# Six instead of four output tiles with the first norm, and the shift's modulation on GpSimd and ScalarE

## The chip, the cores and the metric

The kernel runs on one NeuronCore of a Trainium2 chip. The metric is the device time of one execution in microseconds (us). The engines are TensorE (PE in the profile; PEld is its weight load), VectorE (DVE), ScalarE (ACT), GpSimd (POOL) and SyncE (SP), which here only issues transfers.

## The reference

The program is three layers deep: a block of RWKV-7 and convolution with its feed-forward layer, a forgetting-attention layer and an HGRN2 layer, each with a feed-forward layer behind it. The sequence has 512 tokens and the model 1,024 channels, all in float32. The change touches only the beginning:

```python
mod = jax.nn.silu(c) @ ada_w[l] + ada_b[l]
sh_m, sc_m, gt_m, sh_f, sc_f, gt_f = jnp.split(mod[:, None, :], 6, axis=-1)
h = rms_norm(x, mix_pre_g[l]) * (1.0 + sc_m) + sh_m
p = h @ w_in
p_conv, p_rw = p[..., :2 * CONV_WIDTH], p[..., 2 * CONV_WIDTH:]
prev = jnp.pad(p_rw, ((0, 0), (1, 0), (0, 0)))[:, :-1]
p_rw = p_rw + (prev - p_rw) * rwkv_mu
r, k, v, wd, ad, gd = jnp.split(p_rw, RWKV_SPLITS, axis=-1)
```

So x is normed, scaled per channel by 1 + sc_m (the scale) and moved by sh_m (the shift); both come from a matrix-vector product of `silu(c)` with a 1024x6144 matrix. The result is multiplied by `w_in`.

## The kernel before, in words

Channels lie on the 128 partitions, so the 1,024 channels are eight K tiles of 128x512. A matrix product in float32 precision is made of three: each operand is split into a rounded high part and the low rest, and hi x hi, lo x hi and hi x lo are added up in one accumulator bank of PSUM. The weight of an output tile of 128 channels (128x1024, 512 KB) is loaded to a staging buffer (tile `ws`, three of them), copied by ScalarE to its high part (L168) and subtracted by VectorE to its low part (L169); that is `wload`, L161.

`start` (L332) is the first stage. It squares x and sums it on TensorE (L340, L865), and takes the modulation of each K tile in two: q = 0 is the shift, q = 1 the scale. For K tile 0 TensorE makes both sums (L372). For K tiles 1 to 7 the tile of the transposed matrix (128x1024, one output channel per partition) is loaded by SP (`load`, L360) into one of eight borrowed rooms, and VectorE multiplies it with the broadcast vector `cb` and sums along the row, one instruction of 128x1024 for each q (L375, tiles `ada` and `NM`), then adds the bias (L376). The loads of K tile i + 4 are issued behind the modulation of K tile i.

The loop at L389 then goes over the K tiles. For each, VectorE makes the factor (L393), scales x (L394), ScalarE makes the high part with the shift as bias (L396), VectorE the low part (L397), and TensorE multiplies this K tile into four output tiles at once (L399 to L403): w and a's inputs (number 20), k, r and v of head pair 0 (12, 8, 16). Their accumulators are four banks of PSUM, open over the whole loop. Behind the loop the four are evacuated by `shift_mix` (L408: ScalarE writes a scaled copy, VectorE adds the shifted one).

`mix` (L422) calls `start` at L437 and goes on with `pair(0)` and `pair(1)` (L475). `pair` makes the missing k, r and v tiles of its head pair by `win` (L463, one output tile after the other), then `wkv_prep` (L583), which ends in small score products (L660, L673, L675). `wkv_inverse` (L686) works on GpSimd in 30 small steps (L705, L707) and through DRAM, `wkv_tail` (L765) finishes a pair. The convolution's inputs (`conv_in`, L486) and the gates (L469) are further output tiles of `w_in`. 24 more modulation tiles (L511, `ada_tile`, tile `wa`) are put at the lowest priority.

The order on each engine is not the program's: a scheduler orders the instructions when the kernel is built, by priority (the program's order) and by modelled times; on the chip each engine follows that fixed order and waits on semaphores. Tiles of one tag share their buffers, and a new tile of the tag waits until the old one has been read.

Of the kernel before, what the change touches and what calls it, by code (L numbers as in the profile page):

```python
# [9 lines left out]
F32 = mybir.dt.float32  # L10
F32R = mybir.dt.float32r
# [3 lines left out]
AF = mybir.ActivationFunctionType  # L15
# [4 lines left out]
P = 128  # L20
D = 1024
KD = 8
T1 = 512
# [53 lines left out]
MULT, ADD, SUB = ALU.mult, ALU.add, ALU.subtract  # L77
# [60 lines left out]
def bank(k, ch, *shape):  # L138
    return k.ps[ch].tile([P, *(shape or (512,))], F32, name="s" + ch)
# [21 lines left out]
def wload(k, src, nk, m=P, view=False, hl=None):  # L161

    nc = k.nc
    n = nk * m
    st = k.wst.tile([P, KD * P], F32, name="ws")
    nc.sync.dma_start(st.rearrange("p (n m) -> p n m", m=P) if view else st[:, :n], src)
    hi, lo = hl or [k.whl.tile([P, KD * P], F32R, name=q) for q in ("wh", "wl")]
    nc.scalar.copy(hi[:, :n], st[:, :n])  # L168
    nc.vector.tensor_sub(lo[:, :n], st[:, :n], hi[:, :n])  # L169
    return hi, lo  # L170


def run(steps):
    for _ in steps:
        pass
# [75 lines left out]
def split(k, hi, lo, x):  # L251
    k.nc.scalar.copy(hi, x)  # L252
    k.nc.vector.tensor_sub(lo, x, hi)
# [58 lines left out]
def silu_c(k, pool, sg):  # L312

    nc = k.nc
    k.cb = pool.tile([P, D], F32, name="cb")
    nc.scalar.dma_start(k.cb, k.A["c"].to_broadcast([P, D]))
    nc.scalar.activation(sg, k.cb, AF.Tanh, scale=0.5)
    nc.vector.scalar_tensor_tensor(k.cb, sg, 1.0, k.cb, ADD, MULT)
# [13 lines left out]
def start(k, p1, p2, first):  # L332


    nc, vec = k.nc, k.vec
    mm = nc.tensor.matmul
    x = k.h[:, :, META:T2]
    sq = squares(p2, None, "tmp", T1)
    for i in range(KD):
        add_square(k, sq, i, 0, x[:, i], T1, True)  # L340
    rs = p2.tile([P, T1], F32, name="rs", tag="k2", bufs=1)
    silu_c(k, p1, p2.tile([P, D], F32, name="sgc", tag="tok", bufs=2))
    cs = p1.tile([P, 2 * KD], F32, name="cs")
    sc = cs[:, KD:]
    nc.scalar.activation(cs[:, :KD], vec("c"), AF.Tanh, scale=0.5)
    nc.vector.scalar_tensor_tensor(sc, cs[:, :KD], 1.0, vec("c"), ADD, MULT)
    n = [0]

    def room():
        j = n[0] % 8  # L350
        n[0] += 1
        if j >= 5:
            return k.S.NM[(j - 5) // 2].rearrange("p a b c -> p (a b c)")[:, KD * P * (j % 2):KD * P * (j % 2 + 1)]
        tag, bufs = (("Dm", 1), ("Dt", 1), ("wa", 1), ("tok", 2), ("tok", 2))[j]
        return p2.tile([P, KD * P], F32, name="ada", tag=tag, bufs=bufs)

    ga = p1.tile([P, KD], F32, name="ga")
    ps = bank(k, "b", 2)

    def load(i):  # L360
        rooms[i] = []
        for q in range(2):
            rooms[i].append(room())
            nc.sync.dma_start(rooms[i][q], k.A["ada_w_t"][q] if i == 0 else k.A["ada_wT"][KD * q + i])

    def modulate(i):
        for q in range(2):
            st, nt = rooms[i][q], KD * q + i
            mod = k.mod[:, nt:nt + 1]
            if i == 0:  # L370
                for n in range(KD):
                    mm(ps[:, q:q + 1], st[:, n * P:(n + 1) * P], sc[:, n:n + 1], start=n == 0, stop=n == KD - 1)  # L372
                nc.vector.scalar_tensor_tensor(mod, ps[:, q:q + 1], 0.5, vec("ada_b", nt), MULT, ADD)
            else:
                nc.vector.scalar_tensor_tensor(st, st, 0.5, k.cb, MULT, MULT, accum_out=mod)  # L375
                nc.vector.tensor_add(mod, mod, vec("ada_b", nt))  # L376

    W, rooms = [], {}
    rms_scale(k, sq, 0, T1, rs, True)
    O = [bank(k, c) if c else k.psd.tile([P, 512], F32, name="mm") for c in ("", "", "a", "b")]  # L380
    for w in (1, 0, 2, None, None, 3, None, None):
        if w is not None:
            load(w)
            continue
        i = len(W)
        nt = first[i][0]
        W.append(wload(k, k.A["w_in_t"][nt], KD) if i < 2 else wload(k, k.A["w_in_t"][nt], KD, hl=[
            p2.tile([P, KD * P], F32R, name=f"{q}{i}", tag=q, bufs=2) for q in ("ar", "X")]))
    for i in range(KD):  # L389
        modulate(i)  # L390
        if i + 4 < KD:
            load(i + 4)
        nc.vector.scalar_tensor_tensor(ga[:, i:i + 1], k.mod[:, KD + i:KD + i + 1], 1.0, vec("mix_pre_g", i), ADD, MULT)  # L393
        nc.vector.scalar_tensor_tensor(x[:, i], x[:, i], ga[:, i:i + 1], rs, MULT, MULT)  # L394
        hi, sh = k.x1h[:, i], k.mod[:, i:i + 1]
        nc.scalar.activation(hi, x[:, i], AF.Identity, bias=sh)  # L396
        nc.vector.scalar_tensor_tensor(k.x1l[:, i], x[:, i], sh, hi, ADD, SUB)  # L397
        w = slice(i * P, (i + 1) * P)
        for (h, l), o in zip(W, O):  # L399
            xh, xl = k.x1h[:, i], k.x1l[:, i]  # L400
            mm(o, h[:, w], xh, start=i == 0, stop=False)
            mm(o, l[:, w], xh, start=False, stop=False)
            mm(o, h[:, w], xl, start=False, stop=i == KD - 1)  # L403
    for (nt, evac), o in zip(first, O):
        evac(0, o)


def shift_mix(k, ps, out, nt, m=P):  # L408

    nc = k.nc  # L410
    nc.scalar.activation(out, ps[:m], AF.Copy, scale=k.mu1[:m, nt:nt + 1])
    o = out[:, 1:]
    nc.vector.scalar_tensor_tensor(o, ps[:m, 0:T1 - 1], k.vec("rwkv_mu", nt)[:m], o, MULT, ADD)
# [8 lines left out]
def mix(k):  # L422
    tc, nc, A, vec = k.tc, k.nc, k.A, k.vec
    with ExitStack() as ctx:
        banks(k, ctx, "m", a=3, b=3)
        p1 = ctx.enter_context(tc.tile_pool(name="mx1", bufs=1))
        p2 = ctx.enter_context(tc.tile_pool(name="mx2", bufs=4))
        pd = ctx.enter_context(tc.tile_pool(name="mxd", bufs=1, space=bass.MemoryType.DRAM))
        S = k.S = K()
# [4 lines left out]
        S.wd = p1.tile([P, T1], F32, name="wd")  # L434
        tl0 = [p2.tile([P, T1], F32, name=n, bufs=3 if n == "vx" else 2) for n in ("kx", "rx", "vx")]
        mixed = lambda t, nt: (nt, lambda j, ps: shift_mix(k, ps, t, nt - 8))
        start(k, p1, p2, [mixed(S.wd, 20), mixed(tl0[0], 12), mixed(tl0[1], 8), mixed(tl0[2], 16)])  # L437
        nc.scalar.activation(S.wd[0:64], S.wd[0:64], AF.Tanh)
        S.ka1 = p1.tile([P, 4], F32, name="ka1")
        nc.vector.tensor_scalar(S.ka1, vec("k_a"), -1.0, 1.0, MULT, ADD)  # L440
# [22 lines left out]
        def win(nt, evac):  # L463
            dense(k, A["w_in_t"][nt], k.x1h, k.x1l, SEG1, evac)
# [8 lines left out]
            sigmoid(k, S.gd1, S.gd1)  # L473

        def pair(p):  # L475
            tl = tl0 if p == 0 else []
            for nt, name in ((12 + p, "kx"), (8 + p, "rx"), (16 + p, "vx")):
                if p:
                    t = p2.tile([P, T1], F32, name=name, bufs=3 if name == "vx" else 2)
                    win(*mixed(t, nt))  # L480
                    tl.append(t)
            return wkv_prep(k, p, *tl)
# [365 lines left out]
def squares(pool, acc="ssq", tmp="hf", width=T2, apool=None, **kw):  # L848

    sq = K()  # L850
    sq.apool = apool or pool
    sq.pool, sq.acc, sq.tmp, sq.width, sq.kw = pool, acc, tmp, width, kw
    return sq


def add_square(k, sq, i, c, x, n, pe=False):

    nc = k.nc
    tmp = lambda: sq.pool.tile([P, max(n, H2 + 8)], F32, name="nsq", tag=sq.tmp, **sq.kw)[:, :n]
    if pe:  # L860
        t = tmp()
        nc.scalar.activation(t, x, AF.Square)
        if i == 0:
            sq.ps = bank(k, "a")
        nc.tensor.matmul(sq.ps[:, :n], k.mean, t, start=i == 0, stop=i == KD - 1)  # L865
        return
    if i == 0 and c == 0:
        sq.sum = sq.apool.tile([P, sq.width], F32, name="ssq", tag=sq.acc, bufs=1)
    s = sq.sum[:, c:c + n]
    if i == 0:  # L870
        nc.scalar.activation(s, x, AF.Square)
        return
    t = tmp()
    nc.scalar.activation(t, x, AF.Square)
    nc.vector.tensor_add(s, s, t)


def rms_scale(k, sq, c, n, out, pe=False):

    nc = k.nc  # L880
    if not pe:
        sq.ps = bank(k, "a")
        nc.tensor.matmul(sq.ps[:, :n], k.mean, sq.sum[:, c:c + n], start=True, stop=True)
    s = sq.ps[:, :n]
    y, y2 = (sq.pool.tile([P, max(n, H2 + 8)], F32, name="rsq", tag=sq.tmp, **sq.kw)[:, :n] for _ in range(2))
    newton(k, s, y2, out, 1e-6, k.eps, y)
# [418 lines left out]
def hgrn(k):  # L1305
    tc, nc, A, vec = k.tc, k.nc, k.A, k.vec
    with ExitStack() as ctx:
# [178 lines left out]
        for h in range(KD):  # L1486
            N = K()
            feed = proj(h + 1, N) if h < KD - 1 else iter(())
            for n, steps in enumerate(attend(h, H)):
                if n == 2 and h:  # L1490
                    gated(h - 1, O)
                for _ in range(steps):
                    next(feed, None)
            run(feed)
            O, H = H, N
        gated(KD - 1, O)
        out_proj(k, p2, "hg_out_t", oh, ol, ((3,), (5,)), vec("ffn_norm_2", 8, 16), 2)
# [82 lines left out]
```

## Time and profile before

| | |
|---|---|
| median of 3 runs | 2308.98 us (2307.26 to 2311.26) |
| the profiled execution | 2304.93 us, of which span 2303.2 us |
| TensorE busy | 2235.7 us, 97% of the span |
| VectorE busy | 1429.5 us, 62% |
| ScalarE busy | 979.4 us, 43% |
| GpSimd busy | 100.7 us, 4% |
| mean granted clock of TensorE | 0.986 |

An engine's busy time is the time in which the profile has one of its instructions running. Matmuls are pipelined, and their ends are modelled: at full clock a 128x512 product is shown with 0.39 us, and the next one starts 0.23 us behind it. [...] "Idle before" an instruction is the time in which its engine had nothing running; behind the arrow stands what ended it.

### The profile page before, as it was taken

The page shows a single profiled execution, that of the slowest core. Times are in us where ns is not written, and L with a number is a line of the kernel's source. Part 1 is how long each engine was busy: PE and PEld are TensorE (multiplying, and loading weights), DVE is VectorE, ACT ScalarE, POOL GpSimd, SP SyncE. Part 2 cuts the span into 40 slices and gives each one's busy share as a digit, 9 for nine tenths or more (in the row PEclk, how much of TensorE's full clock was granted, in tenths as well). Part 3 has the DMA queues.
Part 4 walks back from the last instruction along what each step waited for, and adds up shares of the span by engine and source line. Part 5 has one row for each costly group of instructions (what it writes and reads, how often), then busy time and mean ns, then how long its engine had stood idle before and what let it go on. Part 6 is the DMA issues. An engine that isn't in the chain of part 4 may idle for free.

```text
span 2303.2 us, 38001 instructions
## 1 busy us (share of the span) xinstructions
PE 2235.7 (97%) x15280; PEld 1990.0 (86%) x15280; DVE 1429.5 (62%) x3022; ACT 979.4 (43%) x1928; POOL 100.7 (4%) x200
## 2 busy tenths in 40 slices
PE   6999798899999999999999999999999999999999
PEld 4677676688888989888899999999999999999888
DVE  6876777875652566666676666335666667666522
ACT  3535344544442465666553444224333335444321
POOL 1150330000000000000000000000000000000000
PEclk8999999899999999999999999999999999999999
DMA  9443221253233532221032222234111113222332
GB/s 318 152 128 122 76 56 55 88 170 101 92 99 95 148 104 81 67 65 53 33 122 92 86 89 92 83 94 117 56 59 62 45 47 114 92 92 92 91 118 76
DMA packets 73936, 220.11 MB, mean 96 GB/s; under 512 B 8976, under 2 KB 17616, under 8 KB 73760
## 3 DMA queue, kind: packets, MB, share of 16 engines
q1 hardware_dynamic: 68064, 206.17, 28.2%
q0 software_dynamic: 2784, 7.82, 1.5%
q10 hardware_dynamic: 2912, 3.69, 0.5%
q8 instruction: 121, 1.98, 0.4%
q14 instruction: 55, 0.45, 0.1%
HBM read 211.24 MB, written 6.85 MB: 95 GB/s over the span
## 4 chain that ended last, share of the span: by engine, by line
PE 88%; DVE 6%; ACT 3%; DMA 1%; issue 1%; SPq 0%; ACTq 0%; DVEq 0%
PE mm L194 24%; PE mm L193 24%; PE mm L195 23%; PE sb L1402 3%; DVE wl L169 1%; PE sc L1217 1%; PE sb L1192 1%; PE sa L660 1%; ACT wh L168 1%; PE sc L1235 1%; PE sa L865 1%; PE sa L1122 1%; DMA ada<-ada_wT 1%; DMA Dm<-Dd 0%; PE sb L745 0%
## 5 line engine op out<-in xcount | busy, mean ns | idle before, releaser
L193 PE MATMUL mm<-xh,wh 128*128 128x264 f32 (+4 forms) x2852 | 904.8, 317 | 11.0 <-ACT xh L252 5.7
L194 PE MATMUL mm<-xh,wl 128*128 128x264 f32 (+4 forms) x2852 | 895.8, 314 | 4.8 <-DVE wl L169 4.5
L195 PE MATMUL mm<-xl,wh 128*128 128x264 f32 (+4 forms) x2852 | 892.5, 313 | 0.1
L193 PEld LDWEIGHTS mm<-xh,wh 128*128 128x128 f32 x2852 | 536.2, 188 | 46.6 <-ACT xh L252 6.7
L194 PEld LDWEIGHTS mm<-xh,wl 128*128 128x128 f32 x2852 | 536.4, 188 | 39.3 <-DVE wl L169 8.4
L169 DVE TENSOR_TENSOR wl<-ws,wh 128x1024 fp32r<-128x1024 f32 (+3 forms) x358 | 399.9, 1117 | 273.6 <-ACT wh L168 272.8
L195 PEld LDWEIGHTS mm<-xl,wh 128*128 128x128 f32 x2852 | 536.9, 188 | 30.5 <-issue 2.1
L168 ACT CAST wh<-ws 128x1024 fp32r<-128x1024 f32 (+3 forms) x358 | 344.8, 963 | 479.1 <-PE mm L195 410.2
L194 PE MATMUL mm<-gh,wl 128*128 128x264 f32 (+2 forms) x792 | 253.3, 320 | 1.3 <-DVE wl L169 0.9
L193 PE MATMUL mm<-gh,wh 128*128 128x264 f32 (+2 forms) x792 | 252.9, 319 | 0.0
L195 PE MATMUL mm<-gl,wh 128*128 128x264 f32 (+2 forms) x792 | 252.7, 319 | 0.0
L194 PEld LDWEIGHTS mm<-gh,wl 128*128 128x128 f32 x792 | 149.6, 189 | 13.2 <-DVE wl L169 2.8
L193 PEld LDWEIGHTS mm<-gh,wh 128*128 128x128 f32 x792 | 149.5, 189 | 10.5
L195 PEld LDWEIGHTS mm<-gl,wh 128*128 128x128 f32 x792 | 149.6, 189 | 10.2
L975 DVE SCALAR_TENSOR_TENSOR fz<-mm,V,fz 128x511 f32<-128x511 f32 x88 | 65.9, 749 | 63.2 <-ACT fz L973 61.7
L501 DVE SCALAR_TENSOR_TENSOR h<-u,cw,h 128x512 f32<-128x512 f32 x120 | 90.3, 752 | 1.8 <-ACT h L499 0.5
L1402 PE MATMUL sb<-q,kt 128*128 128x64 f32 (+3 forms) x592 | 75.7, 272 | 2.2 <-DVE kt L1434 2.2
L1402 PEld LDWEIGHTS sb<-q,kt 128*128 128x128 f32 x592 | 73.5, 195 | 2.8 <-DVE kt L1434 1.0
L194 PE MATMUL mm<-oh,wl 128*128 128x264 f32 x256 | 74.9, 292 | 0.6 <-DVE wl L169 0.6
L193 PE MATMUL mm<-oh,wh 128*128 128x264 f32 x256 | 74.8, 292 | 0.1
L195 PE MATMUL mm<-ol,wh 128*128 128x264 f32 x256 | 74.4, 291 | 0.0
L973 ACT ACTIVATE fz<-mm,V 128x512 f32<-128x512 f32 x44 | 34.2, 777 | 59.9 <-PE mm L195 59.9
(512 smaller groups left out, 2828.6 us busy)
## 6 DMA issues: line engine op xcount, KB each, us to landing
ws<-w_up_t SPq DMA_DIRECT2D x44, 512.0 KB, 3.5
ws<-gate_t SPq DMA_DIRECT2D x44, 512.0 KB, 3.5
ws<-up_t SPq DMA_DIRECT2D x44, 512.0 KB, 3.5
ws<-down_t SPq DMA_DIRECT2D x34, 512.0 KB, 3.5
wa<-ada_wT SPq DMA_DIRECT2D x32, 512.0 KB, 3.7
ws<-fox_in_t SPq DMA_DIRECT2D x32, 512.0 KB, 3.5
ws<-hg_in_t SPq DMA_DIRECT2D x32, 512.0 KB, 3.5
ws<-w_in_t SPq DMA_DIRECT2D x22, 512.0 KB, 3.8
```

What stands on the lines that cost most here:

```text
L168: nc.scalar.copy(hi[:, :n], st[:, :n])
L169: nc.vector.tensor_sub(lo[:, :n], st[:, :n], hi[:, :n])
L193: mm(o, hi[:, w], xh[i][:, a:b], start=start and i == 0, stop=False)
L194: mm(o, lo[:, w], xh[i][:, a:b], start=False, stop=False)
L195: mm(o, hi[:, w], xl[i][:, a:b], start=False, stop=stop and i == n - 1)
L501: nc.vector.scalar_tensor_tensor(acc, src, w, acc, MULT, ADD)
L660: nc.tensor.matmul(sc[hh][:, kind], lt[r, cs], ar[r, c], start=True, stop=True)
L865: nc.tensor.matmul(sq.ps[:, :n], k.mean, t, start=i == 0, stop=i == KD - 1)
L973: nc.scalar.activation(z, ps, AF.Identity, bias=vec("ffn_dw_b", nt), scale=wt(2))
L975: nc.vector.scalar_tensor_tensor(z[:, t:], ps[:, 0:T1 - t], wt(2 - t), z[:, t:], MULT, ADD)
L1122: nc.tensor.matmul(s, k.blk, sq[:, hs(j)], start=True, stop=True)
L1402: nc.tensor.matmul(o, kt[:, a:a + P], qv, start=True, stop=True)
```

## The change

Two more output tiles, k and r of head pair 1 (13 and 9), join the K loop. Their accumulators are two more banks, so all eight banks of PSUM are in use in the stage. Their weights are loaded and split at i = 1 and i = 2, in halves of 128x512, into buffers borrowed from tiles that are needed later (`ys`, `y1`, `u`, `kk`, `tl`). Their products run three K tiles behind the others (`late(i - LAG)`), and the last three K tiles' products come when the first four tiles have been evacuated. `pair(1)` then makes only v by `win`. The modulation of the shift (q = 0) of K tiles 1 to 7 is made by GpSimd, which multiplies the tile with `cb` in place, and ScalarE, which sums it in a copy with the factor 0.5; the scale (q = 1) stays on VectorE.

```diff
@@ start, modulate
-            else:
+            elif q:
                 nc.vector.scalar_tensor_tensor(st, st, 0.5, k.cb, MULT, MULT, accum_out=mod)
                 nc.vector.tensor_add(mod, mod, vec("ada_b", nt))
+            else:
+                nc.gpsimd.tensor_tensor(st, st, k.cb, op=MULT)
+                nc.scalar.activation(st, st, AF.Copy, scale=0.5, accum_out=mod)
+                nc.vector.tensor_add(mod, mod, vec("ada_b", nt))
@@ start
-    O = [bank(k, c) if c else k.psd.tile([P, 512], F32, name="mm") for c in ("", "", "a", "b")]
+    O = [bank(k, c) if c else k.psd.tile([P, 512], F32, name="mm") for c in ("", "", "a", "b", "a", "b")]
+    half = KD * P // 2
+
+    def halves(tags):
+
+        return [p2.tile([P, half], F32R, name="wx", tag=t, bufs=2 if t in ("ys", "y1", "u") else 1) for t in tags]
+
+    def late(i):
+
+        for (h, l), o in zip(W[4:], O[4:]):
+            (h, l), w = (t[i * P // half] for t in (h, l)), slice(i * P % half, i * P % half + P)
+            mm(o, h[:, w], k.x1h[:, i], start=i == 0, stop=False)
+            mm(o, l[:, w], k.x1h[:, i], start=False, stop=False)
+            mm(o, h[:, w], k.x1l[:, i], start=False, stop=i == KD - 1)
+
...
+    LAG = 3
     for i in range(KD):
         modulate(i)
         if i + 4 < KD:
             load(i + 4)
+        if i in (1, 2):
+            st = k.wst.tile([P, KD * P], F32, name="ws")
+            nc.sync.dma_start(st, k.A["w_in_t"][first[3 + i][0]])
+            hl = [halves(t) for t in ((("ys", "ys"), ("y1", "y1")) if i == 1 else (("u", "u"), ("kk", "tl")))]
+            for j in range(2):
+                split(k, hl[0][j], hl[1][j], st[:, half * j:half * j + half])
+            W.append(hl)
...
-        for (h, l), o in zip(W, O):
+        for (h, l), o in zip(W[:4], O):
...
-    for (nt, evac), o in zip(first, O):
+        if i >= LAG:
+            late(i - LAG)
+    for n, ((nt, evac), o) in enumerate(zip(first, O)):
+        if n == 4:
+            for i in range(KD - LAG, KD):
+                late(i)
         evac(0, o)
@@ mix
-        start(k, p1, p2, [mixed(S.wd, 20), mixed(tl0[0], 12), mixed(tl0[1], 8), mixed(tl0[2], 16)])
+        tl1 = [p2.tile([P, T1], F32, name=n, bufs=2) for n in ("kx", "rx")]
+        start(k, p1, p2, [mixed(S.wd, 20), mixed(tl0[0], 12), mixed(tl0[1], 8), mixed(tl0[2], 16), mixed(tl1[0], 13), mixed(tl1[1], 9)])
@@ pair
-            tl = tl0 if p == 0 else []
-            for nt, name in ((12 + p, "kx"), (8 + p, "rx"), (16 + p, "vx")):
-                if p:
+            tl = (tl0, tl1)[p] if p < 2 else []
+            for n, (nt, name) in enumerate(((12 + p, "kx"), (8 + p, "rx"), (16 + p, "vx"))):
+                if n >= len(tl):
```

## Rows read from the trace of the kernel before

**Rows 1.** The page: span, and TensorE's busy time, share and instructions.
```profile
span 2303.2 us, 38001 instructions
...
PE 2235.7 (97%) x15280; PEld 1990.0 (86%) x15280; DVE 1429.5 (62%) x3022; ACT 979.4 (43%) x1928; POOL 100.7 (4%) x200
```

**Rows 2.** Busy time by stretch: from:to, length, engines (instructions), clock, DMA share, GB/s.
```profile
22.90:55.00 32.10, 23.35 (x80) 16.22 (x81) 31.86 (x65) 9.63 (x12) 3.62 (x2) 0.81 0.94 338
...
59.10:83.00 23.90, 22.65 (x112) 17.11 (x113) 21.75 (x48) 15.67 (x26) 0.00 (x0) 1.00 0.51 163
83.00:143.00 60.00, 57.14 (x321) 40.46 (x322) 48.52 (x103) 26.54 (x68) 24.30 (x40) 1.00 0.48 142
143.00:241.00 98.00, 97.66 (x714) 72.61 (x715) 67.04 (x134) 40.15 (x95) 30.65 (x57) 0.95 0.39 120
```

**Rows 3.** VectorE in time order, the stage's ends: start, us, engine, line, operation.
```profile
22.62 0.16 DVE L373 SCALAR_TENSOR_TENSOR mod<-sb,V 128x1 f32<-128x1 f32 x1 [2.42 <-PE sb L372]
...
53.37 1.62 DVE L397 SCALAR_TENSOR_TENSOR xl<-h,mod,xh 128x512 fp32r<-128x512 f32 x2
57.71 0.75 DVE L413 SCALAR_TENSOR_TENSOR wd<-mm,V,wd 128x511 f32<-128x511 f32 x1 [2.72 <-ACT wd L411]
```

**Rows 4.** TensorE in time order: first product, two neighbours at full clock, last.
```profile
28.25 0.80 PE L401 MATMUL mm<-xh,wh 128*128 128x512 f32 x1 [5.67 <-ACT xh L396]
...
51.50 0.39 PE L401 MATMUL sb<-xh,ar 128*128 128x512 f32 x1
51.73 0.40 PE L402 MATMUL sb<-xh,X 128*128 128x512 f32 x1
...
58.64 0.39 PE L403 MATMUL sb<-xl,ar 128*128 128x512 f32 x1
```

**Rows 5.** Groups by line and shape to 62 us: count, busy us, mean ns, idle before.
```profile
L375 DVE SCALAR_TENSOR_TENSOR ada<-ada,cb 128x1024 f32<-128x1024 f32 x8 | 9.8, 1219 | 2.5 <-DMA ada<-ada_wT 2.5
...
L375 DVE SCALAR_TENSOR_TENSOR NM<-NM,cb 128x1024 f32<-128x1024 f32 x6 | 7.3, 1219 | 0.0
...
L451 POOL MEMSET NM<- 128x2048 f32 x2 | 3.6, 1809 | 43.9 <-DVE NM L375 43.7
...
L317 ACT ACTIVATE sgc<-cb 128x1024 f32<-128x1024 f32 x1 | 1.1, 1057 | 1.2 <-DMA cb<-c 1.2
```

**Rows 6.** GpSimd and VectorE in time order, both busy, about 113 us.
```profile
113.17 0.68 DVE L643 TENSOR_TENSOR k<-k,pin 128x512 f32<-128x512 f32 x1
113.21 0.81 POOL L707 TENSOR_TENSOR Tb<-Tb,tm 64x60 f32<-64x60 f32 x1
...
113.77 0.81 DVE L632 TENSOR_TENSOR ar<-kk,G 128x512 f32<-128x512 f32 x1
```

**Rows 7.** VectorE in time order: the same line with GpSimd idle.
```profile
79.74 0.69 DVE L632 TENSOR_TENSOR ar<-kk,G 128x512 f32<-128x512 f32 x1
```

**Rows 8.** GpSimd in time order, not held up by VectorE.
```profile
310.14 0.21 POOL L705 TENSOR_TENSOR tm<-Gb,Tb 64x15 f32<-64x15 f32 x1 [2.26 <-DMA Gb<-Ld]
...
315.86 0.29 POOL L705 TENSOR_TENSOR tm<-Gb,Tb 64x64 f32<-64x64 f32 x1
```

**Rows 9.** Groups by line and shape, ScalarE: reading out a sum.
```profile
L1203 ACT ACTIVATION_READ_ACCUMULATOR pr<-pr,st 128x1 f32 x64 | 12.0, 187 | 0.0
```

**Rows 10.** SP's queue in time order: start, us until issued, what.
```profile
31.52 6.59 SPq L364 DMA_DIRECT2D NM<-ada_wT  x3
```

**Rows 11.** DMA issues to 60 us: count, size, median us to landing.
```profile
NM<-ada_wT SPq DMA_DIRECT2D x6, 512.0 KB, 7.7
```

**Rows 12.** The chain that ended last, in time order: start, us, what.
```profile
82.91 1.11 PE sa L660 x8
...
173.47 1.51 PE sa L799 x16
...
205.20 1.06 PE sa L660 x8
```

**Rows 13.** TensorE's waits between 55 and 300 us: total, times, longest.
```profile
PE sb L723 <- DMA Dm<-Dd: 10.3, 1, 10.3
```

More of the change, by code (lines that the diff above doesn't have):

```diff
@@ L373, in modulate @@
                 nc.vector.scalar_tensor_tensor(mod, ps[:, q:q + 1], 0.5, vec("ada_b", nt), MULT, ADD)
-            else:
-                nc.vector.scalar_tensor_tensor(st, st, 0.5, k.cb, MULT, MULT, accum_out=mod)
+            elif q:
+                nc.vector.scalar_tensor_tensor(st, st, 0.5, k.cb, MULT, MULT, accum_out=mod)
+                nc.vector.tensor_add(mod, mod, vec("ada_b", nt))
+            else:
+                nc.gpsimd.tensor_tensor(st, st, k.cb, op=MULT)
+                nc.scalar.activation(st, st, AF.Copy, scale=0.5, accum_out=mod)
                 nc.vector.tensor_add(mod, mod, vec("ada_b", nt))
```

## The prediction

> **What bounds the kernel now.** I read the page first: TensorE is busy 97% of the span [rows 1]. So nearly everything is a question of where TensorE is *not* doing useful work, and the table of busy time by stage shows where that is near the change. In the stage of the first norm (22.9 to 55.0 us) VectorE is busy 31.86 of 32.1 us and TensorE 23.35, at a granted clock of 0.81; behind it TensorE is busy 22.65 of 23.9, 57.14 of 60 and 97.66 of 98 us, and VectorE 91%, 81% and 68% [rows 2]. The reader is to see two regimes: up to 55 us VectorE sets the pace, from 59 to 241 us TensorE does.
>
> The time-ordered rows of VectorE give the stage its ends: it runs without a gap from 22.8 us (a last wait of 2.42 us for the matrix-vector products ends at 22.62) to the last low part of x at 53.37 + 1.62 = 55.0 us, and waits for TensorE next only before 57.71 [rows 3]. TensorE's own rows: the first product of the four tiles starts at 28.25, the last at 58.64 (over at 59.0), and at full clock one follows another in 0.23 us [rows 4]. The four tiles are 4 x 8 x 3 = 96 products, 22.3 us of work at 0.232 us, in 30.8 us. The hole that the change wants to fill is the other 8.5 us.
>
> **The change part by part.**
>
> *1. Seven shift tiles leave VectorE.* Fourteen multiply-and-sum operations of 1.22 us stand in the stage [rows 5]; back to back one costs 1.15 us (the next starts while its sum is read). Seven go. One of them, K tile 1's, lies before the packed stretch and is worth nothing there; six in it give 6 x 1.15 = 6.9 us.
>
> *2. Two weight splits enter the stage.* Four subtractions of 128x512, each as the 0.68 us operation at 113.17 whose successor starts 0.60 later [rows 6]: 4 x 0.60 = +2.4 us on VectorE here, and 2 x 1.15 us less in the stage behind. By these two parts alone VectorE would finish at 55.0 - 6.9 + 2.4 = 50.5 us.
>
> *3. Seven products of 128x1024 on GpSimd.* GpSimd is idle from 6 us until 49.8 [rows 5], so its own time looks free. The trace has no GpSimd operation of this size; it has them at 64 elements, beside VectorE operations with two operands in SBUF. There the two take turns: GpSimd's operation at 113.21 ends (114.02) only after VectorE's of 113.17 does (113.85), and VectorE's next, at 113.77, lasts 0.81 us [rows 6] where the same line took 0.69 with GpSimd idle [rows 7]. So a GpSimd operation of 60 to 64 elements holds VectorE for 0.12 us, some 1.9 ns an element. Alone, 15 elements take GpSimd 0.21 us and 64 take 0.29 [rows 8], 1.6 ns an element. For 1,024 elements that is 1.6 to 2.0 us; I take 2.0 of holding, by the rows with both engines busy. Every large VectorE operation of this stage (the sums, the scaling of x, its low part, the splits) has two operands in SBUF. Bounds: 0 if a long operation shares freely, 2.1 at 0.12 us for 60 elements.
>
> [...]
>
> So on VectorE's clock a shift tile costs 2.0 where it cost 1.15. Six in the packed stretch: +12.0, less about half of the 2.42 us wait before 22.62 [rows 3], in which the second of them can run: -1.2. VectorE ends at 50.5 + 12.0 - 1.2 = **61.3 us** instead of 55.0.
>
> *4. Seven ScalarE passes with a sum.* 1.06 us for 128x1024 [rows 5] and 0.19 for reading the sum [rows 9]: 7 x 1.25 = 8.7 us, and four half casts of some 0.6, half of that row and its fixed share. ScalarE is busy 9.63 of 32.1 us there [rows 2]; cover enough, and nobody else reads the result until the tile's own shift is added. Cost 0; without that cover up to 1.2 us behind each wait.
>
> *5. SP's queue.* Two more weight loads go in, ahead of the loads for i = 6 and 7 and behind a staging buffer that a split must free; what queues behind them is these modulation loads. 1.05 MB at the stage's 338 GB/s is 3.1 us. The last modulation loads were issued by 31.52 + 6.59 = 38.1 us [rows 10] and land in 7.7 [rows 11], at 45.8, some 5 us before VectorE used them (its last scalings and low parts end at 55.0). With VectorE 6 us later the slack grows: 0, at worst 3.1. Two loads leave the stage behind. GpSimd's queue: the clearing of the mask buffers and of u's edge stand behind the seven products; the first is needed behind the score products of 82.91 [rows 12], the other later: 0.
>
> *6. TensorE.* 48 products move forward: 11.1 us. When the four tiles end, 96 + 30 = 126 of the 144 products are done: 29.2 us, which from 28.25 ends at 57.5 at full clock, so VectorE sets the end, not TensorE. Before, the last product ended 4.0 us after the last low part of x, with two K tiles queued; with the K tiles further apart some 14 products should be left, 3.2: 61.3 + 3.2 = **64.5 us** for the four tiles, 5.5 later than now. The 18 products left over follow, 18 x 0.232 = 4.2, in the time in which TensorE would wait for the tanh of wd anyway: six tiles are done at **68.7**. Before, the same work was done at 59.0 + 11.1 = 70.1. The sum is **-1.4 us**.
>
> *7. Held buffers.* The two tiles' weights lie in buffers of the first head pair, and one accumulator bank stays taken until 68.7. Those buffers are needed again late in pair 0's preparation, shortly before its score products at 82.91 [rows 12]: 0.
>
> *8. What is late next.* wd, k, r and v of the first pair start 5.5 us later, so those score products come at about 88. TensorE doesn't stand meanwhile if the products of the next tiles (v of pair 1, the convolution inputs, the gates) are issued ahead of them; there is work for 30 us. Later the chain has slack: pair 0's tail is over at 175, pair 2's scores, which need its buffers, start at 205.20 [rows 12]. So TensorE's progress carries to the end, and I keep -1.4. If the cover fails, up to 5.5 + 1 comes on top.
>
> The profiled execution took 2304.93 us (span 2303.2, 1.7 around it), 4.05 under the median of the three runs, 2308.98. The sum makes 2303.5 of it; against the median, **2307.5 us**. About 0.2%, 4.6 us, is what a measurement can tell from no change here.
>
> **The rivals.**
> *Faster: GpSimd and VectorE share freely at this size* (part 3 at 0). VectorE ends at 50.5; TensorE then sets the end, 28.25 + 29.2 and about 3 us at the lower clock = 60.5 for the four tiles, 64.7 for six: -5.4, so 2303.5. For it: the holding is seen at 64 elements only. Against it: it is seen every time that both are busy. 25%.
>
> *Slower: the first pair's chain is late where the issue order has it early.* TensorE's order is fixed, whatever GpSimd holds up. If the small products of pair 0 stand in it where they would come by 59 us plus the same steps, TensorE waits there, up to 5.5 us and 1 more for the bank of part 7, against 1.4 gained: -1.4 + 6.5 = +5.1, 2314. It decides once over 6.0 us of waiting is not covered for a loss past 4.6, over 1.4 for any loss. For it: TensorE waited 10.3 us for one DMA of pair 2's chain [rows 13], so the order is not proof against late chains. Against: only 4.1 us of idle between 59 and 143 [rows 2]. 25%.
>
> *The two tiles don't get there in time:* their weights land or are split after TensorE's turn, and the late products hold up the others. 3.1 us of part 5 uncovered: +1.7, 2310.5. 5%.
>
> **How the numbers follow.** My forecast has 45%, its own range 2302 to 2311: six holdings of 1.6 to 2.1 us instead of 2.0 give -2.4 to +0.6, and a new order of issue may move most of the 4.1 us that TensorE idles between 59 and 143, 3 either way. Faster by over 0.2% (under 2304.4): 0.7 of the first rival and 0.22 of the forecast, 0.28. Slower (over 2313.6): 0.7 of the second and 0.1 of the forecast, 0.22. Within: 0.50. The range takes in the first rival with a little more, 2300, and the second to 2315.
>
> **What would show it right or wrong.** Right: GpSimd's products last 2 us or more; VectorE operations that start under them last 2 to 3 us instead of 0.75 or 1.22; the last low part of x ends near 61 us, the first four tiles near 64.5, six near 69; no new wait over 3 us between 64 and 140. Wrong: VectorE's durations are unchanged and it ends near 50 us (first rival); TensorE waits for pair 0's scores between 80 and 110 us (second); the late products wait for splits (third).

## The result, and the profile after

The kernel after takes 2331.22 us (median of four runs, 2328.61 to 2333.19), the kernel before 2309.49 in the same comparison: a ratio of 1.0100 [1.0077, 1.0122], 21.7 us slower. The forecast was 2307.5, its range ended at 2315. The profiled execution shown here took 2333.18 us, 2 above its median; that of before lay 4 below its own, so the two spans differ by 28.2 us, and sums below are made against medians.

The page of the kernel after, span and TensorE, which answers to [rows 1]:

```profile
span 2331.4 us, 38018 instructions
...
PE 2245.2 (96%) x15280; PEld 1997.3 (86%) x15280; DVE 1433.9 (62%) x3010; ACT 986.7 (42%) x1944; POOL 118.0 (5%) x207
```

Busy time by stretch of the kernel after (columns as in [rows 2]; the clock is TensorE's granted one, 1.00 being full):

```profile
22.90:55.00 32.10, 21.04 (x60) 13.49 (x61) 31.83 (x41) 14.33 (x21) 14.01 (x6) 0.69 0.91 324
...
83.00:143.00 60.00, 42.25 (x224) 28.48 (x222) 38.15 (x82) 21.87 (x49) 23.36 (x38) 0.87 0.39 114
143.00:241.00 98.00, 97.07 (x709) 73.42 (x709) 66.62 (x135) 39.83 (x104) 19.02 (x42) 0.94 0.36 106
...
120.00:140.00 20.00, 5.37 (x35) 2.54 (x33) 10.24 (x17) 3.24 (x5) 16.53 (x30) 0.70 0.17 34
```

The first stage looks as forecast: VectorE full, GpSimd busy for 14 us. The surprise is 83 to 143 us: TensorE is busy 42.25 us where it was 57.14 [rows 2], and most of the hole lies in 120 to 140, with 5.37 busy of 20.

TensorE of the kernel after in time order: the last product of the four tiles, of the six, the first product of the first pair's chain (wd's), and the place of the hole; the last line is from its waits (total, times, longest):

```profile
68.83 0.39 PE L429 MATMUL sb<-xl,ar 128*128 128x512 f32 x1
...
74.38 0.39 PE L397 MATMUL sb<-xl,wx 128*128 128x512 f32 x1
74.70 0.69 PE L629 MATMUL sa<-wd,wlr 64*128 64x512 f32 x1
...
143.19 2.05 PE L755 MATMUL sb<-Dm,NM 128*128 128x128 f32 x8 [17.82 <-DMA Dm<-Dd]
...
148.35 0.74 PE L692 MATMUL sa<-ar,kk 64*128 64x256 f32 x4
...
PE sb L755 <- DMA Dm<-Dd: 31.5, 3, 17.8
```

VectorE of the kernel after, around the same time:

```profile
127.77 0.67 DVE L668 TENSOR_TENSOR kk<-kk,pin 128x512 f32<-128x512 f32 x1
...
149.55 0.45 DVE L695 COPY_PREDICATED NM<-cm,sa 128x256 f32<-128x256 uint8 x1 [19.31 <-PE sa L692]
```

TensorE stands for 17.82 us before the first product of the first pair's inverse (L755, L723 of before), whose data GpSimd works out and a DMA brings. Behind it in TensorE's order stand the second pair's score products (L692, L660 of before). Their last operand was ready at 127.77 + 0.67 = 128.4 us; they run at 148.35, and VectorE, which needs them, stands for 19.31. In the kernel before the order is the other way round: the second pair's score products begin at 117.50 us, the last of them and the inverse follow, without a wait:

```profile
130.42 0.70 PE L660 MATMUL sa<-ar,kk 64*128 64x256 f32 x4
...
136.17 1.05 PE L723 MATMUL sb<-Dm,NM 128*128 128x128 f32 x8
```

The inverse's data come later too. GpSimd's DMA issues of the first pair's inverse, in the kernel before:

```profile
98.14 0.95 POOL L696 DMA_DIRECT2D Ld<-NM  x1 [44.54 <-DVE LM L664]
...
128.96 0.92 POOL L715 DMA_DIRECT2D Dm<-Dd  x1 [1.52 <-DMA Dd<-Tb]
```

and in the kernel after:

```profile
106.73 0.96 POOL L728 DMA_DIRECT2D Ld<-NM  x1 [31.77 <-DVE LM L696]
...
138.24 0.92 POOL L747 DMA_DIRECT2D Dm<-Dd  x1 [1.50 <-DMA Dd<-Tb]
```

They are 8.6 and 9.3 us later. A late chain was foreseen, in the slower rival as a wait of at most 6.5 us; a block of ready work behind the wait was not.

### The profile page after: what moved, and what is told of

It is laid out like the page before. It is cut to its first block, busy times and chain, and to the rows that moved or that the text cites. A ratio compares the mean times of both kernels' runs of the same rounds, so it can differ in the third digit from the quotient of the medians.

```text
span 2331.4 us, 38018 instructions
## 1 busy us (share of the span) xinstructions
PE 2245.2 (96%) x15280; PEld 1997.3 (86%) x15280; DVE 1433.9 (62%) x3010; ACT 986.7 (42%) x1944; POOL 118.0 (5%) x207
## 4 chain that ended last, share of the span: by engine, by line
PE 87%; DVE 5%; DMA 3%; ACT 3%; POOL 1%; issue 1%; ACTq 0%; SPq 0%; POOLq 0%; DVEq 0%
PE mm L194 23%; PE mm L193 23%; PE mm L195 23%; PE sb L1434 3%; PE sc L1249 1%; PE sa L692 1%; PE sb L1224 1%; DVE wl L169 1%; PE sc L1267 1%; ACT wh L168 1%; POOL Tb L739 1%; DMA Dm<-Dd 1%; POOL tm L737 1%; PE sa L1154 1%; PE sa L897 1%
## 5 line engine op out<-in xcount | busy, mean ns | idle before, releaser
L169 DVE TENSOR_TENSOR wl<-ws,wh 128x1024 fp32r<-128x1024 f32 (+4 forms) x356 | 397.3, 1116 | 276.1 <-ACT wh L168 275.4
L168 ACT CAST wh<-ws 128x1024 fp32r<-128x1024 f32 (+4 forms) x356 | 342.6, 962 | 480.4 <-PE mm L195 415.5
L195 PEld LDWEIGHTS mm<-gl,wh 128*128 128x128 f32 x792 | 149.7, 189 | 10.3
L193 PE MATMUL mm<-oh,wh 128*128 128x264 f32 x256 | 74.8, 292 | 0.0
```

The source lines that it names most:

```text
L193: mm(o, hi[:, w], xh[i][:, a:b], start=start and i == 0, stop=False)
L195: mm(o, hi[:, w], xl[i][:, a:b], start=False, stop=stop and i == n - 1)
```

## The experiments

Three theories. **1, the issue order**: the loss is TensorE standing before the inverse because ready score products stand behind it. **2, the holding**: GpSimd's products hold VectorE, and that lateness alone is the loss, wherever TensorE waits. **3, the borrowed buffers** of the fifth and sixth tile hold up the first pair.

**The order undone, in the kernel after.** `issue_after` places the block's instructions behind the named one in their engine's order and adds no wait:

```diff
-        wkv_inverse(k, Q[0])
+        with tc.issue_after(Q[1].last.ins):
+            wkv_inverse(k, Q[0])
@@ wkv_prep
-    nc.tensor.matmul(bo, k.blk, rk, start=True, stop=True)
+    Q.last = nc.tensor.matmul(bo, k.blk, rk, start=True, stop=True)
```

> The kernel after, with one thing more: the first pair's inverse is issued behind the second pair's preparation, so that on TensorE the second pair's score products stand ahead of the first products of that inverse, as in the kernel before. Theory 1 (issue order: the loss is TensorE standing 17.8 us before an inverse product while ready score products stand behind it): the wait shrinks below 4 us and 12 to 17 us come back, 2314 to 2319 us. Theory 2 (GpSimd's holding of VectorE carries the whole loss, wherever TensorE waits): the wait moves to other products and the time stays within 3 us of the kernel after, about 2331. Theory 3 (the borrowed buffers): about 2331 as well.

Measured: 2316.63 us, 1.0028 [1.0012, 1.0045] of before (2309.68 in this and the next three comparisons; over all comparisons the median of before lies between 2309.49 and 2311.23, so a difference of two kernels from different comparisons is good to some 2 us). 14.6 us come back. The first pair's inverse starts at 151.23 without a wait:

```profile
151.23 1.05 PE L756 MATMUL sb<-Dm,NM 128*128 128x128 f32 x8
```

Theory 1 by its numbers. But 6.9 us over before are left, which this one edge does not explain. In the profile two things stand beside them, not tested apart: TensorE waits 6.60 us before the fourth pair's inverse where before waits 1.86, and between 130 and 140 us it runs at a granted clock of 0.50.

**GpSimd's part alone, in the kernel before.**

```diff
-            else:
+            elif q:
                 nc.vector.scalar_tensor_tensor(st, st, 0.5, k.cb, MULT, MULT, accum_out=mod)
                 nc.vector.tensor_add(mod, mod, vec("ada_b", nt))
+            else:
+                nc.gpsimd.tensor_tensor(st, st, k.cb, op=MULT)
+                nc.scalar.activation(st, st, AF.Copy, scale=0.5, accum_out=mod)
+                nc.vector.tensor_add(mod, mod, vec("ada_b", nt))
```

> The kernel before with the shift's modulation tiles multiplied by GpSimd and summed by ScalarE, and nothing else; four output tiles in the first stage. Theory 1: VectorE's last low part ends about 4 to 6 us later than before (seven products of 2.4 held against seven operations of 1.2 removed), the order on TensorE is that of before, and the time is 3 to 8 us above the kernel before, 2312 to 2317. Theory 2: nearly all the loss is here, 2326 to 2331. Theory 3: within 3 us of the kernel before.

Measured: 2314.36 us, 1.0020 [1.0006, 1.0034]: 4.7 us. VectorE's last low part of x ends at 59.50 + 0.75 = 60.25, 5.2 later than in [rows 3], and is now held up by ScalarE's cast as well:

```profile
59.50 0.75 DVE L401 SCALAR_TENSOR_TENSOR xl<-h,mod,xh 128x512 fp32r<-128x512 f32 x1 [0.79 <-ACT xh L400]
```

With four tiles the holding costs what the stage shows, and not 20 us. Theory 2 falls as the whole cause. TensorE keeps the order of before, the last score products of the second pair ahead of the inverse, and does not wait there:

```profile
134.21 0.59 PE L664 MATMUL sa<-ar,k 64*128 64x256 f32 x2
...
146.35 1.05 PE L727 MATMUL sb<-Dm,NM 128*128 128x128 f32 x8
```

**Six tiles alone, in the new order and in the old one.** The kernel after with the shift back on VectorE (the diff above reversed), and the same with the order undone as in the first experiment.

> The kernel after with the shift's modulation tiles back on VectorE, so that the six output tiles stay and GpSimd and ScalarE do nothing for the shift. VectorE's last low part should end near 57.4 us (55.0 and four splits of 0.6), six tiles near 66. Theory 1: a wait before the first pair's inverse stays, as that inverse stands early in the issue order here too; 2309 to 2325. Theory 2: at or below the kernel before, 2304 to 2309, and no wait over 5 us before the inverse. Theory 3: near the kernel after, 2328 to 2332.

> The six output tiles with the shift on VectorE, and the first pair's inverse issued behind the second pair's preparation. Theory 1: no wait over 4 us before that inverse; TensorE has the two tiles' products about 4 us earlier than before (66 against 70), so 2304 to 2308 us. Theory 2: the same as the run without the moved inverse within 3 us. Theory 3: near 2330.

Measured: 2319.62 us, 1.0039 [1.0025, 1.0053], and 2301.36 us, 0.9966 [0.9954, 0.9978]. The one edge is worth 18.3 us, and the second kernel is 2.6 us below the range expected of it. TensorE with the inverse ahead (here the first of four groups of the second pair's scores had run before the wait), in time order and as a stretch:

```profile
138.66 1.62 PE L751 MATMUL sb<-Dm,NM 128*128 128x128 f32 x6 [13.10 <-DMA Dm<-Dd]
140.53 1.22 PE L688 MATMUL sa<-ar,kk 64*128 64x256 f32 x2
...
140.00:160.00 20.00, 20.00 (x67) 14.81 (x66) 7.60 (x16) 3.82 (x14) 0.00 (x0) 0.50 0.09 27
```

and with the inverse behind the scores:

```profile
124.44 0.70 PE L689 MATMUL sa<-ar,kk 64*128 64x256 f32 x2
...
139.92 1.13 PE L752 MATMUL sb<-Dm,NM 128*128 128x128 f32 x8 [0.97 <-DMA Dm<-Dd]
...
140.00:160.00 20.00, 19.97 (x209) 15.63 (x210) 15.23 (x24) 7.33 (x20) 11.62 (x21) 1.00 0.46 149
```

The wait shrinks from 13.10 to 0.97 us. A further cost is in the last row of each: behind the wait TensorE is busy 20 of 20 us, but at a granted clock of 0.50, and gets through 67 records; the other run, at 1.00, through 209, smaller ones among them. A pair of score products takes 1.22 us instead of 0.70. (In the kernel before, 128x512 products follow one another in 0.43 us from 42.2 to 45.0 us, at a clock of 0.50, and in 0.23 from 36.0 to 39.6, at 1.00.) What share of the other 6 of the 18.3 us this is was not measured by itself. Nor does every stand cost that: behind its wait of 17.82 us the kernel after is soon back at 1.00:

```profile
145.00:150.00 5.00, 4.75 (x26) 3.64 (x25) 0.45 (x2) 1.74 (x3) 0.00 (x0) 0.65 0.02 3
150.00:155.00 5.00, 5.00 (x35) 3.92 (x34) 4.69 (x12) 1.97 (x7) 0.00 (x0) 1.00 0.00 0
```

Theory 3 falls: with the same borrowed buffers the six tiles are 8.3 us faster than before. And the six tiles are what turned the order: they have the inverse ahead without GpSimd's part, and GpSimd's part without them does not. Why the scheduler chose so is open.

The medians so far, in us:

| | four tiles, order of before | six tiles, inverse behind the scores | six tiles, inverse ahead |
|---|---|---|---|
| shift on VectorE | 2309.7 (before) | 2301.4 | 2319.6 |
| shift on GpSimd and ScalarE | 2314.4 | 2316.6 | 2331.2 (after) |

From before to after: -8.3 for the six tiles, +18.3 for the order, +11.6 for GpSimd, together +21.6. That is one way through the table, and the parts do not simply add: the order costs 18.3 or 14.6, GpSimd's part 4.7 with four tiles, 15.3 or 11.6 with six. Why it is dearer with six is in part open (see the kernel with both edges).

**The order turned, in the kernel before.** The inverse is written as a generator that stops behind its first four products; it is begun ahead of the second pair, whose score products are placed behind them; the four transfers that fill `Dd` for it move ahead with it. Core of the edit:

```diff
         Q[0] = pair(0)
+        inv = wkv_inverse_steps(k, Q[0])
+        S.first = next(inv)
         Q[1] = pair(1)
...
-        wkv_inverse(k, Q[0])
+        run(inv)
@@ wkv_prep, around the score products
+        with k.tc.issue_after(S.first.ins) if p == 1 else nullcontext():
```

> The kernel before (four tiles, the shift on VectorE) with only the issue order changed: the first four products of the first pair's inverse stand ahead of the second pair's score products, as in the kernel after. Theory 1: TensorE waits there some 10 to 16 us for the inverse's data and the time is 8 to 16 us above the kernel before, 2317 to 2326. Theories 2 and 3 (holding, borrowed buffers): within 3 us of the kernel before.

Measured: 2321.79 us, 1.0060 [1.0042, 1.0079], 11.6 over before (2310.22 here and in the next three). TensorE:

```profile
122.62 0.40 PE L194 MATMUL mm<-xh,wl 128*32 128x512 f32 x1
135.91 2.05 PE L733 MATMUL sb<-Dm,NM 128*128 128x128 f32 x8 [12.89 <-DMA Dm<-Dd]
137.89 1.23 PE L663 MATMUL sa<-ar,kk 64*128 64x256 f32 x4
```

With nothing of the change in it, the order alone makes a wait of 12.89 us. The kernel after has 17.82: 4.9 more, for a chain that is 8 to 9 us later. Here, too, the clock is back soon, at 0.98 from 140 to 145 us.

**The late products put last, in the kernel after.** `LAG = KD` instead of 3: the fifth and sixth tile's products all stand behind the first four tiles'.

> The kernel after, with all products of the fifth and sixth tile behind the first four tiles' (lag of eight K tiles instead of three). The first four tiles should end near 64.8 us instead of 69.2, six near 75 as now. Theory 1: the first pair's chain starts 4 us earlier, TensorE arrives at its inverse as before, so the 17.8 us wait shrinks to 13 to 14 and the time falls by 3 to 6 us, to 2325 to 2328. Theory 2 (VectorE's holding alone counts, the interleaving doesn't): 2330 to 2332.

Measured: 2332.10 us, 1.0108 [1.0083, 1.0132]; the wait is 17.85 us; the 3 to 6 us expected did not come. TensorE:

```profile
65.09 0.39 PE L429 MATMUL sb<-xl,ar 128*128 128x512 f32 x1
...
74.00 0.69 PE L629 MATMUL sa<-wd,wlr 64*128 64x512 f32 x1
```

The four tiles do end 3.7 us earlier. But the chain's first product, wd's, stands behind the late products in the order, and comes at 74.00 where it came at 74.70, though ScalarE had its input (the tanh of wd) ready at 68.3. The earlier tiles feed nothing: the same mechanism at another place.

**What holds VectorE.** In the kernel before, GpSimd works on the dead shift tile: it clears it for odd K tiles, multiplies it for even ones.

```diff
+                if q == 0 and i % 2:
+                    nc.gpsimd.memset(st, 0.0)
+                elif q == 0:
+                    nc.gpsimd.tensor_tensor(st, st, k.cb, op=MULT)
```

> The kernel before; after VectorE has summed a shift tile, GpSimd also works on the dead 128x1024 tile: on odd K tiles it clears it (it writes only), on even ones it multiplies it by the broadcast vector (two operands read). If any GpSimd work of this size holds VectorE, VectorE operations of 0.75 and 1.22 us that start under either become 2.8 to 3.4 us; if only an operation that reads the same memory does, those under the clearing keep 0.75 and 1.22 and only those under the products grow; if it were GpSimd's writes alone, both grow. The time should be within 0 to 6 us above the kernel before, two or three products held.

Measured, in one execution: 2310.83 us. GpSimd in time order:

```profile
16.14 0.95 POOL L378 MEMSET ada<- 128x1024 f32 x1 [10.12 <-DVE ada L375]
25.05 2.34 POOL L380 TENSOR_TENSOR ada<-ada,cb 128x1024 f32<-128x1024 f32 x1 [7.95 <-DVE ada L375]
...
41.41 3.33 POOL L380 TENSOR_TENSOR ada<-ada,cb 128x1024 f32<-128x1024 f32 x1 [5.71 <-DVE mod L376]
```

VectorE under them:

```profile
16.20 1.22 DVE L375 SCALAR_TENSOR_TENSOR ada<-ada,cb 128x1024 f32<-128x1024 f32 x1
...
25.00 0.68 DVE L572 SCALAR_TENSOR_TENSOR rsq<-sa,rsq 128x512 f32<-128x512 f32 x1
25.60 2.86 DVE L375 SCALAR_TENSOR_TENSOR NM<-NM,cb 128x1024 f32<-128x1024 f32 x1
...
41.31 1.22 DVE L375 SCALAR_TENSOR_TENSOR ada<-ada,cb 128x1024 f32<-128x1024 f32 x1
```

Under the clearing VectorE keeps its 1.22 us. Under the product its sum of 25.60 lasts 2.86. The operation of 25.00, one operand of which is in PSUM, was running when that product began, and the product keeps its 2.34. The product of 41.41, begun behind a VectorE sum of two SBUF operands, itself takes 3.33: in both cases the one that began second was held.

**The same edge for the third pair.** The kernel of six tiles, shift on VectorE, first inverse moved, has one more such wait, 7.35 us at 251 us, as the kernel before has one of 10.25 [rows 13]. Ready behind it stand products of the fourth pair's last input tile. `k.vend` is the last product of that tile (in the first of the two kernels it is an entry of a table of tile ends):

```diff
-        wkv_inverse(k, Q[2])
+        with tc.issue_after(k.vend.ins):
+            wkv_inverse(k, Q[2])
```

> The six output tiles with the shift on VectorE and the first pair's inverse behind the second pair's preparation, and one more edge of the same kind: the third pair's inverse is issued behind the last input tile of the fourth pair, whose products stood ready behind its 7.35 us wait at 251 us. Theory 1 (what costs is ready work standing behind a waiting product): that wait falls under 2.5 us, 4 to 6 us come back, 2295 to 2298 us. Rival (the pair's chain sets the end, TensorE only waits for it): the wait moves to later products of that chain and the time stays within 2 us of 2301.

Measured: 2292.03 us, 0.9929 [0.9914, 0.9944]. 9.3 us on top, more than the wait and than the 4 to 6 us expected; three waits of 0.85 to 1.35 us stay. The rival falls: the chain did not set the end.

By itself in the kernel before:

> The kernel before with only one edge: the third pair's inverse issued behind the last input tile of the fourth pair. Its wait of 10.25 us at 260 us should fall under 4 us. If that edge is worth by itself what it brought on top of the six tiles (9.3 us), 2299 to 2304 us; if it only works with the six tiles (because then the pairs are further ahead), within 3 us of the kernel before.

Measured: 2297.67 us, 0.9941 [0.9927, 0.9955] (before 2311.23 here and in the next two): 13.6 us, again more than expected. The edge needs none of the change; the inverse starts without a wait:

```profile
261.91 1.14 PE L725 MATMUL sb<-Dm,NM 128*128 128x128 f32 x8
```

**GpSimd's part with both edges,** that is, the kernel after with both inverses moved.

> The kernel after (six tiles, the shift on GpSimd and ScalarE) with both inverses moved behind the ready products. Beside the same kernel with the shift on VectorE (2292.0 us) it measures what GpSimd's holding costs once no order stands in the way: if only the 6 to 7 us by which VectorE and the six tiles end later, 2298 to 2302 us; if the later chain lets TensorE's clock fall as well, as in the run with one edge, 2303 to 2309 us; if the holding is hidden by the following stage, 2291 to 2295 us.

Measured: 2304.88 us, 0.9966 [0.9954, 0.9979], 12.9 above the same kernel with the shift on VectorE (11.8 when each is set against the kernel before of its own comparison). In the profiles the chain's first product is 9.4 us later (76.65 against 67.29), the fourth pair's first scores 8.4 (281.96 against 273.52), the next norm's first product 14.5 (392.68 against 378.19). So the stage's lateness is carried nearly in full, and some 6 us come later, from a longer wait for the fourth pair's inverse, at

```profile
330.42 2.08 PE L758 MATMUL sb<-Dm,NM 128*128 128x128 f32 x8 [4.91 <-DMA Dm<-Dd]
```

where the other kernel waits 2.30 us, and from the clock: 0.92 granted between 241 and 470 us instead of 0.95. How the two share those 6 us is open.

**A shorter lag.** `LAG = 2`, six tiles, shift on VectorE, both inverses moved.

> Six tiles, the shift on VectorE, both inverses moved, and the fifth and sixth tile two K tiles behind the first four instead of three, so that 12 instead of 18 of their products stand between the last of the four tiles and the first product of the first pair's chain. If the start of that chain still counts, it comes 1 to 1.5 us earlier and the time is 2289 to 2291 us; if not, 2291 to 2294 us; if the new order brings a product ahead of its data again, a wait over 4 us shows between 60 and 145 us and the time is above 2296 us.

Measured: 2289.42 us, 0.9913 [0.9897, 0.9929]. Its executions (2288.73 to 2299.79) overlap those of the version with three (2289.79 to 2295.69), so a gain over that is not shown, and the chain's first product comes no earlier (67.84 us), so neither is the reason given for one. Its median is the lowest here, 21.8 us under before.

## Why the prediction was wrong

**Parts 1 to 4, VectorE: right in kind, 2 us short.** GpSimd's products in the kernel after:

```profile
29.25 2.48 POOL L378 TENSOR_TENSOR NM<-NM,cb 128x1024 f32<-128x1024 f32 x1 [5.85 <-DMA NM<-ada_wT]
34.40 6.13 POOL L378 TENSOR_TENSOR ada<-ada,cb 128x1024 f32<-128x1024 f32 x2 [2.67 <-DMA ada<-ada_wT]
```

and VectorE there:

```profile
29.43 2.85 DVE L420 SCALAR_TENSOR_TENSOR h<-h,ga,rs 128x512 f32<-128x512 f32 x1
...
34.89 3.41 DVE L169 TENSOR_TENSOR X<-ws,ar 128x1024 fp32r<-128x1024 f32 x1
...
62.57 0.75 DVE L423 SCALAR_TENSOR_TENSOR xl<-h,mod,xh 128x512 fp32r<-128x512 f32 x1 [0.79 <-ACT xh L422]
```

Operations of 0.74 and 1.22 us take 2.85 and 3.41; five are held so, by 2.05 to 2.2 us each, 10.6 in all where 12.0 less 1.2 was put down. A product that is not held itself takes 2.34 to 2.49 us, not 2.0. VectorE ends at 63.3 instead of 61.3: 0.79 of it is the wait for ScalarE's cast, which part 4 costed at nothing; the other 1.2 us was not traced. So the turns that the rows show at 64 elements are seen at 1,024 too, and the clearing above, which only writes, held nothing: VectorE kept its 1.22 us under it.

**Part 6, the tiles: failed by its own order.** Four tiles end at 69.2 instead of 64.5 and six at 74.8 instead of 68.7, where the equal work of before would have ended at 70.1. 2 us are VectorE's. For the four tiles the rest is that 24 of the late products stand between those of the four, which I had counted as done in TensorE's pauses; with them put last the four end at 65.5. That the leftover products run while TensorE "would wait for the tanh" held only for a part of them. The tanh of wd is ready at 71.85 + 0.63 = 72.48 us:

```profile
71.85 0.63 ACT L470 ACTIVATE wd<-wd 64x512 f32<-64x512 f32 x1
```

The rest of them stand ahead of wd's product in the order, and it runs at 74.70, 2.2 us later (62.65 before).

**Part 8 is the step that failed.** "TensorE doesn't stand meanwhile", and "I keep -1.4". I read the slack of the chain from the trace of before, in that kernel's order. The change gave the kernel another order, in which the first pair's inverse stands ahead of the second pair's scores. That alone is 11.6 us in the kernel before, and 14.6 and 18.3 in two kernels with six tiles. It is not all: with that order undone the kernel is still 6.9 us over before, where -1.4 was forecast. The -1.4 is part 6's: TensorE was to have the six tiles done 1.4 us ahead of the equal work of before, and is 4.7 us behind (74.8 against 70.1). That such lateness of the stage reaches the end is seen with GpSimd's part alone (5.2 us late in the stage, 4.7 in the time) and with both edges; that it makes up the 6.9 is argued from its size, not tested.

**The slower rival named the mechanism and priced it wrong.** "TensorE's order is fixed" was right. The place was not: it looked for the wait at the first pair's scores, and those ran at 90.93 us, 8 later than before, without a wait. And its price, 5.5 us of lateness and 1 more, supposes that a wait costs by how much the chain is late. The wait is as long as the time from TensorE's arrival until the data land (125.37 to 143.19 us in the kernel after), and with ready work behind it its cost is of that size, here less and there more (17.82 us of wait were worth 14.6, 12.89 cost 11.6, 12.1 were worth 18.3). The evidence was in [rows 13]: a stand of 10.3 us in a kernel in which nothing was late. Moving that one product is worth 13.6 us.

**The faster rival** (free sharing) fell by the rows of 29.43 and 34.89. The weights were in time (third rival): the late products wait for a split 0.20 us at most. Part 7's buffers cost nothing that shows.

## What to carry to other kernels

TensorE, which ran here in a fixed order, paid for long waits with work that stood ready behind them: moving one inverse was worth 14.6 us at a wait of 17.82, 18.3 at 12.1 us less of waiting and 13.6 at a wait of 10.25. So look at each long wait for what the next instructions needed and when that was ready, and move the waiting one behind them. When a change makes a planner order the work anew, the slack read from the old trace need not hold: compare the two orders at the slow chains before any arithmetic on busy times. And an idle GpSimd was no free place for a product beside a VectorE that read two operands from SBUF: five of 128x1024 held it for 2.05 to 2.2 us each.

## What the hardware showed that I had not expected

The price of a stand was not its length here. Behind the 13.10 us wait TensorE was busy from 140 to 160 us at a granted clock of 0.50, and removing 12.1 us of waiting brought 18.3; moving the 10.25 us wait of the kernel before brought 13.6. But behind the waits of 17.82 and 12.89 us the clock was back within some 5 us (1.00 from 150 us, 0.98 from 140), and there 14.6 and 11.6 us were at stake, less than the waits. What decides between the two is open.

GpSimd's clearing of 128x1024 (0.95 us) left VectorE undisturbed at 1.22 us, its product of the same size held it for 2.05 to 2.2 us in the kernel after and made 2.86 us of 1.22 in the probe, and it was held in turn (3.33 instead of 2.34 us) when VectorE was first.
